# Lower probabilities times upper values on two column halves of TensorE, all eight key tiles of a half head in one stretch

## The chip, the cores and the metric

The kernel runs on one core of a Trainium2 chip. The metric is the device time of one execution in microseconds (us); lower is better. Before the change the median of three runs is 2208.74 us (2208.42 to 2209.5).

Engines are written as in the profile: PE is TensorE (PEld its weight loads), DVE VectorE, ACT ScalarE, POOL GpSimd, SP SyncE.

## The reference

Two layers, each an attention-and-convolution mixer followed by a gated feed-forward block, on one sequence of 1024 tokens with 1024 channels. The change lies in the attention of the mixer: 8 heads, queries and keys of 64 + 32 channels, values of 64 channels.

```
sc = (jnp.einsum("bqhd,bkhd->bhqk", qn, k_nope)
      + jnp.einsum("bqhr,bkr->bhqk", qr, k_rope))
p = jax.nn.softmax(sc.astype(jnp.float32) * scale, axis=-1).astype(v.dtype)
return jnp.einsum("bhqk,bkhd->bqhd", p, v)
...
u = a * jax.nn.sigmoid(gt)
u = _dwconv(u, w_dw_conv[l], b_dw_conv[l])
```

The second fragment is a depthwise convolution of 31 taps on 512 channels. The part of its taps that is left over when the attention begins (50 per layer) is computed beside the attention.

## The kernel before, in words

Attention is written out by hand in `attention` as a chain of 64 steps per layer (8 heads times 8 query tiles of 128), software-pipelined over steps. For step n TensorE's own order is:

- `values` (L1823): probabilities times values. A half head is 512 queries of one head; its 1024 keys are eight key tiles, and quarter c handles key tiles 2c and 2c+1 in one step. The four quarters of half head g stand in steps 4g+4 to 4g+7. The result `o` is one PSUM bank of 128 partitions by 512 queries.
- `turn(n)` (L1800 to L1803): eight 128x128 transposes on PE put a pair of finished probability tiles `p` into two PSUM banks `t`; ACT writes the upper part `pt` in f16 (L1802) and DVE the remainder, the lower part (L1803). So every half head has an upper and a lower `pt`.
- `scores(n+2)` (L1760): six matmuls into one of two double banks `s`; DVE takes the row maximum (L1762), and ACT the exponential (L1770, `expo(n+1)`, one step later) into `p`.

Values are also held as an upper and a lower f16 part, side by side in one weight tile of 128 columns (`v`, L1746 to L1749): for an even head columns 0 to 63 are the upper values (`main`) and 64 to 127 the lower ones (`aux`); for an odd head the other way round. One matmul of `pt` against that tile therefore yields upper values on 64 partitions of `o` and lower values on the other 64. After the last quarter ACT scales one half of `o` out of PSUM (L1829) and DVE adds the other half to it (L1830): the two halves are summed in any case.

In the step after a finished head `sums` (L1841) transposes eight columns of row sums on PE: a weight tile of 128 by 8, and DVE takes the reciprocals (L1843).

Beside this run the leftover taps (`tap_late`). `LATE_KINDS` (L83) gives each tap its kind, in a pattern of five that differs between the first and the second half of the list: `act` is two ACT instructions of half a tile (L1991), `pool` one product on POOL (L1994), and both then add through an accumulating DMA that POOL issues (L1999); `both` is a product and an addition on POOL (L1997). `LATE_COST` spreads the list over steps 0 to 56, each kind taking a share in proportion to its cost. When all taps are in, POOL sums the four channel blocks (L2005, `conv_total`), and ACT and DVE split the sum at the end (L2009, `conv_split`).

PE, DVE, ACT and POOL each execute their instructions in this written order.

Of the kernel before, what the change touches and what calls it, by code (L numbers as in the profile page):

```python
# [79 lines left out]
ROW_LATE = {0: (6,)}  # L80
E = mybir.EngineType
MANUAL = [E.PE, E.DVE, E.Activation, E.Pool, E.SP]
LATE_KINDS = (("act", "both", "pool", "act", "pool"), ("pool", "both", "pool", "pool", "pool"))  # L83
LATE_COST = {"act": 1.1, "pool": 3.5, "both": 4.8}
NEAR_TAPS = (12, 14, 15, 14)
NEAR_ORDER = (0, 1, 2, 3)
# [52 lines left out]
class Encoder:  # L139
# [1583 lines left out]
    def attention(self, l, u, conv, away, spill, kvs, loaded, ahead, wo, begun):  # L1723
        nc = self.nc
# [3 lines left out]
        state, v, vts = {}, [], {}  # L1728
# [79 lines left out]
        def values(group, c, n):  # L1808
            h, gg = divmod(group, 2)
            st = state[h]  # L1810
            e = h % 2
            main, aux = slice(e * 64, e * 64 + 64), slice(64 - e * 64, 128 - e * 64)
            if c == 0:
                if gg == 0 and e == 0:
                    st["y"], st["rb"] = self.blk(f"yt{l}_{h}"), self.blk(f"rb{l}_{h}")
                elif gg == 0:
                    st["y"], st["rb"] = state[h - 1]["y"], state[h - 1]["rb"]
                st["po", gg] = self.bank(f"o{l}_{h}_{gg}")
            y, rb, po = st["y"], st["rb"], st["po", gg] if c < 3 else st.pop(("po", gg))
            pt = st["pt"][gg][c // 2]  # L1820
            for s in range(2):
                for i in range(2):
                    nc.tensor.matmul(po, v[2 * c + i][:, h // 2, e, :], pt[s][:, 2 * (c % 2) + i, :],  # L1823
                                     start=(c == 0 and i == 0 and s == 0), stop=(c == 3 and i == 1 and s == 1))
            if c < 3:
                return
            st["pt"].pop(gg)
            qs = HALVES[gg]
            nc.scalar.activation(out=y[main, qs], in_=po[aux, :], func=AF.Copy, scale=vr[aux, 0:1])  # L1829
            nc.vector.scalar_tensor_tensor(out=y[main, qs], in0=po[main, :], scalar=vr[main, 0:1], in1=y[main, qs], op0=ALU.mult, op1=ALU.add)  # L1830
            if h < HEADS - 2 and gg:
                agenda[n + 1].append(lambda: sums(h, main, st, y, rb))
            elif h == HEADS - 1:
                if gg:
                    divide(y[main, qs], main, gg)
                else:
                    agenda[n + 1].append(lambda: (divide(y[main, qs], main, gg), finish(last, y, 0)))

        def sums(h, main, st, y, rb):
            pr = self.bank(f"sr{l}_{h}", (8, 128))  # L1840
            nc.tensor.transpose(pr, st["sums"], self.ident)  # L1841
            rs = self.cp.tile([8, 128], F32, name=f"rs{l}_{h}", tag="rs", bufs=2)
            nc.vector.reciprocal(out=rs, in_=pr)  # L1843
            nc.sync.dma_start(out=sd[h].rearrange("(a b) -> a b", a=8), in_=rs)
            nc.sync.dma_start(out=rb[main, :], in_=sd[h:h + 1].partition_broadcast(64))
            if h == HEADS - 2:
                for c, cs in enumerate(HALVES):
                    agenda[LAST_MULT[c]].append(lambda cs=cs: nc.vector.scalar_tensor_tensor(out=y[main, cs], in0=y[main, cs], scalar=1.0, in1=rb[main, cs], op0=ALU.mult, op1=ALU.mult))
            elif h % 2:
                agenda[h * 8 + 10 + Y_DELAY].append(lambda: nc.gpsimd.tensor_tensor(out=y, in0=y, in1=rb, op=ALU.mult))  # L1850
                agenda[h * 8 + 10 + Y_DELAY + (Y_SPLIT if h < 5 else Y_LAST)].append(
                    lambda: ys.append(self.split(y, f"ys{l}_{h}", on_pool=True)))
# [9 lines left out]
        def divide(ym, main, q):  # L1862
            nc.vector.tensor_tensor(out=ym, in0=inv[q][main, :], in1=ym, op=ALU.mult)
# [10 lines left out]
        def finish(h, y, c):  # L1874
            cs = HALVES[c]
            if c == 0:
                ys.append([self.blk(f"ys{l}_{h}{i}", F32R) for i in "hl"])
            hi, lo = (t[:, cs] for t in ys[-1])
            nc.scalar.copy(out=hi, in_=y[:, cs])
            nc.vector.scalar_tensor_tensor(out=lo, in0=y[:, cs], scalar=1.0, in1=hi.bitcast(F32), op0=ALU.mult, op1=ALU.subtract)  # L1880

        ys, inv, po = [], {}, begun["po"]
# [3 lines left out]
        while any(rest.values()):  # L1886
            j = max((j for j in rest if rest[j]), key=lambda j: (all(j != e for e, _ in late[-2:]), len(rest[j]), -j))
            late.append((j, rest[j].pop(0)))
        kinds = [LATE_KINDS[2 * i // len(late)][i % 5] for i in range(len(late))]
        costs, taken = [LATE_COST[kind] for kind in kinds], set()  # L1890
# [33 lines left out]
        for n in range(-2, total + 2):  # L1924
            if n == total - 2:
                expo(n + 1)
            for g, c in chain.get(n, ()):
                values(g, c, n)
# [9 lines left out]
            if n + 2 < total:  # L1938
                h, qt = divmod(n + 2, 8)
# [14 lines left out]
            if n == total:  # L1954
                values(2 * HEADS - 1, 0, n)
                values(2 * HEADS - 1, 1, n)
                early(1, range(2, 3))
                values(2 * HEADS - 1, 2, n)
                values(2 * HEADS - 1, 3, n)
# [180 lines left out]
```

## Time and profile before

| | |
|---|---|
| median of three runs | 2208.74 us |
| the profiled execution | 2208.39 us |
| its span, first to last instruction | 2206.6 us |
| granted TensorE clock | 0.999 |
| PE busy | 2196.8 us |
| DVE busy | 1831.5 us |
| ACT busy | 1468.9 us |
| POOL busy | 592.7 us |
| attention chain of layer 0 | about 210 to 409 us of the span |
| attention chain of layer 1 | about 1304 to 1503 us of the span |

Busy times are of the whole span; the attention chains are two stretches of about 200 us in which the balance between the engines is a different one. A matmul's recorded time runs from its start to its modelled end, and successive matmuls overlap, so what a matmul costs in a dense row is read from one start to the next.

### The profile page before, as it was taken

Reading aid. Unit: us, or ns where it says so; the run is one execution under the profiler, and the core shown is the slowest. Engines: PE = TensorE matmul, PEld = TensorE weight load, DVE = VectorE, ACT = ScalarE, POOL = GpSimd, SP = SyncE. Lnnn points to the kernel's source line nnn. Section 1 sums busy time; section 2 is a strip of 40 time slices with the busy share of each in tenths; the row PEclk is TensorE's granted clock in tenths of the full one; section 3 lists DMA queues with packets and bytes.
Section 4 is the critical chain, followed back from the end, with each engine's and each line's share of the span. In section 5 each row is a group of like instructions: output and inputs, shape, how many; then the busy total and the mean of one; then the engine's idle time right before and its main releaser. Section 6 shows DMA issues by size and latency. Waiting matters only on the chain.

```text
span 2206.6 us, 29859 instructions
## 1 busy us (share of the span) xinstructions
PE 2196.8 (100%) x10770; PEld 1320.0 (60%) x10770; DVE 1831.5 (83%) x2506; ACT 1468.9 (67%) x2207; POOL 592.7 (27%) x546
## 2 busy tenths in 40 slices
PE   9999999999999999999999999999999999999998
PEld 8887666784444444644488876667744444446445
DVE  7989888778988887787859788887798888878877
ACT  6455987746898886554623569786468887865544
POOL 1221799511121111000012227983111111110000
PEclk9999999999999999999999999999999999999999
DMA  6896887954588886554558968789646988856533
GB/s 193 165 176 176 167 166 156 289 141 115 137 243 257 223 258 155 191 170 155 167 134 168 192 151 176 154 182 237 169 104 143 258 240 241 239 142 218 183 116 120
DMA packets 163269, 400.96 MB, mean 182 GB/s; under 512 B 22144, under 2 KB 30192, under 8 KB 163120
## 3 DMA queue, kind: packets, MB, share of 16 engines
q0 software_dynamic: 67136, 154.28, 37.8%
q1 hardware_dynamic: 95696, 244.24, 32.5%
q8 instruction: 84, 1.38, 0.3%
q10 hardware_dynamic: 288, 0.53, 0.1%
q14 instruction: 65, 0.53, 0.1%
HBM read 270.75 MB, written 69.66 MB: 154 GB/s over the span
## 4 chain that ended last, share of the span: by engine, by line
PE 97%; DVE 1%; ACT 1%; issue 0%; DMA 0%; DVEq 0%; ACTq 0%
PE p L1251 36%; PE pd L1496 17%; PE po L985 7%; PE s L1760 7%; PE o L1823 5%; PE t L1800 5%; PE pq L239 3%; PE pa L239 3%; PE pg L239 2%; PE pkv L239 2%; PE pg L557 2%; PE pn L239 1%; PE pk L239 1%; PE pa L557 1%; PE pv L1736 1%; PE pu L239 1%
## 5 line engine op out<-in xcount | busy, mean ns | idle before, releaser
L1251 PE MATMUL p<-b,w 128*128 128x512 f16 x3696 | 804.0, 379 | 0.0
L1251 PEld LDWEIGHTS <-w 128*128 128x128 f16 x3696 | 361.6, 99 | 427.4 <-issue 1.1
L1496 PE MATMUL pd<-ab,wd 128*128 128x512 f16 (+2 forms) x1920 | 404.2, 373 | 0.0
L1142 POOL DMA_DIRECT2D wu<-in_w_up x176 | 152.6, 881 | 743.2 <-DVE w L1215 540.3
L1496 PEld LDWEIGHTS <-wd 128*128 128x128 f16 x1656 | 161.9, 98 | 179.4 <-issue 0.5
L1803 DVE SCALAR_TENSOR_TENSOR pt<-t,pt 128x512 f16<-128x512 f32 x256 | 163.8, 681 | 34.8 <-ACT pt L1802 33.7
L1760 PE MATMUL s<-k,q 96*128 96x512 f16 x768 | 186.9, 379 | 0.0
L1215 DVE SCALAR_TENSOR_TENSOR w<-wu,wf,w 128x512 f16<-128x512 f32 (+1 forms) x216 | 177.2, 834 | 3.9 <-ACT w L1212 3.9
L1994 POOL TENSOR_TENSOR late<-gate,par 128x1016 f32<-128x1016 f32 (+11 forms) x79 | 170.9, 2164 | 0.0
L1802 ACT ACTIVATE pt<-t 128x512 f16<-128x512 f32 x256 | 139.1, 597 | 45.9 <-PE t L1800 45.2
L1212 ACT ACTIVATE w<-wu,wf 128x512 f16<-128x512 f32 (+1 forms) x216 | 164.8, 781 | 0.1
L1762 DVE TENSOR_REDUCE mx<-s 128x1 f32<-128x1024 f32 x128 | 155.3, 1213 | 0.0
L1485 ACT ACTIVATE ab<-ac,ds 128x512 f16<-128x512 f32 x108 | 75.5, 716 | 108.5 <-DVE ac L1400 72.9
L1770 ACT ACTIVATE p<-s,mx 128x1024 f32<-128x1024 f32 x128 | 143.4, 1121 | 1.2 <-DVE mx L1762 0.8
L1977 DVE SCALAR_TENSOR_TENSOR conv<-gate,par,conv 128x1009 f32<-128x1009 f32 (+14 forms) x110 | 139.8, 1274 | 3.5 <-ACT conv L641 0.8
L1800 PEld LDWEIGHTS t<-ident,p 128*128 128x128 f32 x1024 | 120.0, 141 | 25.7 <-ACT p L1770 1.1
L1800 PE MATMUL t<-ident,p 128*128 128x128 f32 x1024 | 133.4, 273 | 0.6 <-ACT p L1770 0.6
L1823 PE MATMUL o<-pt,v 128*128 128x512 f16 x512 | 130.8, 379 | 0.0
L1708 DVE SCALAR_TENSOR_TENSOR o<-zg,par,o 128x1023 f32<-128x1023 f32 x88 | 112.7, 1281 | 8.9 <-ACT o L1702 7.4
L1259 DVE SCALAR_TENSOR_TENSOR zg<-p,wf,zg 128x512 f32<-128x512 f32 x72 | 54.0, 750 | 72.0 <-PE p L1251 62.3
L1760 PEld LDWEIGHTS <-q 96*128 96x128 f16 x768 | 74.1, 97 | 64.5 <-issue 2.1
L1708 DVE SCALAR_TENSOR_TENSOR v<-zv,par,v 128x1023 f32<-128x1023 f32 x88 | 112.1, 1276 | 0.0
(2173 smaller groups left out, 3936.7 us busy)
## 6 DMA issues: line engine op xcount, KB each, us to landing
wu<-in_w_up SPq DMA_DIRECT2D x98, 512.0 KB
wu<-in_w_up POOLq DMA_DIRECT2D x176, 256.0 KB, 4.8
sd<-in_w_down SPq DMA_DIRECT2D x44, 512.0 KB
ws<-sd SPq DMA_DIRECT2D x44, 512.0 KB
act<-v SPq DMA_DIRECT2D x36, 512.0 KB
ac<-act SPq DMA_DIRECT2D x72, 256.0 KB
wo<-in_w_o POOLq DMA_DIRECT2D x64, 256.0 KB, 7.4
x_mix<-y SPq DMA_DIRECT2D x32, 256.0 KB
```

The source lines that it names most:

```text
L239: nc.tensor.matmul(ps[:, HALVES[c]], w, x[:, HALVES[c]], start=(k == 0 and s == 0), stop=(k == n - 1 and s == 2))
L1212: nc.scalar.activation(out=t, in_=src, func=AF.Copy, scale=scale[f])
L1215: nc.vector.scalar_tensor_tensor(out=t, in0=src, scalar=scale[f], in1=hi, op0=ALU.mult, op1=ALU.subtract)
L1251: nc.tensor.matmul(ps, w[p][:, k * 128:(k + 1) * 128], b[:, q], start=(i in (1, 5, 2) and k == 0 and t == 0), stop=(k == 3 and t == 2), sk ...
L1496: nc.tensor.matmul(ps[t, m][:, cs], w[i, j][p][:, m * 128:(m + 1) * 128], b[:, q, cs], start=(i in (1, 5, 2) and j == 0 and s == 0), stop= ...
L1708: self.nc.vector.scalar_tensor_tensor(out=o[:, a:b], in0=z[:, at + a:at + b], scalar=self.par[l][:, tap:tap + 1], in1=o[:, a:b], op0=ALU.m ...
L1760: nc.tensor.matmul(ps[:, cs], q[0:96, i, qs], k[0:96, j, cs], start=(s == 0), stop=(s == 2))
L1762: nc.vector.tensor_reduce(out=mx, in_=ps, op=ALU.max, axis=AX.X, negate=True)
L1800: nc.tensor.transpose(tp[:, i, qi * 128:(qi + 1) * 128], st["p"][2 * qp + qi][:, kt * 128:(kt + 1) * 128], self.ident)
L1803: nc.vector.scalar_tensor_tensor(out=lo, in0=tp, scalar=P_SCALE, in1=hi, op0=ALU.mult, op1=ALU.subtract)
L1823: nc.tensor.matmul(po, v[2 * c + i][:, h // 2, e, :], pt[s][:, 2 * (c % 2) + i, :], start=(c == 0 and i == 0 and s == 0), stop=(c == 3 and ...
L1994: self.nc.gpsimd.tensor_tensor(out=p[:, lo:hi], in0=u[:, lo + s:hi + s], in1=self.tap(l, j, t).broadcast_to([128, hi - lo]), op=ALU.mult)
```

## The change

`values` no longer multiplies the lower probabilities in each quarter. Each quarter only has its two matmuls with the upper `pt` (both parts of the values). In the last quarter of a half head eight matmuls follow with the lower `pt`, one per key tile, and only with the upper values: 64 weight columns instead of 128. Even key tiles write partitions 0 to 63 of `o`, odd ones 64 to 127, that is, two halves of the array's columns in turn. The product of lower probabilities and lower values is left out. Separately, one of five taps in the second half of the list changes from POOL's product to ACT's.

```
-LATE_KINDS = (("act", "both", "pool", "act", "pool"), ("pool", "both", "pool", "pool", "pool"))
+LATE_KINDS = (("act", "both", "pool", "act", "pool"), ("act", "both", "pool", "pool", "pool"))
...
-            for s in range(2):
-                for i in range(2):
-                    nc.tensor.matmul(po, v[2 * c + i][:, h // 2, e, :], pt[s][:, 2 * (c % 2) + i, :],
-                                     start=(c == 0 and i == 0 and s == 0), stop=(c == 3 and i == 1 and s == 1))
+            for i in range(2):
+                nc.tensor.matmul(po, v[2 * c + i][:, h // 2, e, :], pt[0][:, 2 * (c % 2) + i, :],
+                                 start=(c == 0 and i == 0), stop=False, skip_group_check=True)
+            if c == 3:
+                for kt in range(8):
+                    rows = slice(kt % 2 * 64, kt % 2 * 64 + 64)
+                    nc.tensor.matmul(po[rows], v[kt][:, h // 2, e, main], st["pt"][gg][kt // 4][1][:, kt % 4, :],
+                                     start=False, stop=(kt >= 6), skip_group_check=True)
```

On PE, around the last quarter of the first half head (step 7 of layer 0), the order before is this; `pt_01` is the upper and `pt_11` the lower part of key tiles 4 to 7, and each matmul row stands twice, for two key tiles.

```order
L1760 MATMUL s_1_0_1902<-k_1_1686,q_1_1685 128x512
L1823 LDWEIGHTS v_6_1701
L1823 MATMUL o_0_0_1813<-pt_01_1715,v_6_1701 128x512
...
L1823 MATMUL o_0_0_1813<-pt_11_1716,v_6_1701 128x512
L1800 MATMUL t_0_30_1924<-ident,p_0_6_1876 128x128 x2
```

And now, at the same place; `pt_10` is the lower part of key tiles 0 to 3, `v_0` to `v_6` are the values of two key tiles each, and each matmul row stands twice here too.

```order
L1760 MATMUL s_1_0_1896<-k_1_1686,q_1_1685 128x512
L1822 MATMUL o_0_0_1813<-pt_01_1715,v_6_1701 128x512
L1827 LDWEIGHTS v_0_1593
L1827 MATMUL o_0_0_1813<-pt_10_1714,v_0_1593 64x512
L1827 MATMUL o_0_0_1813<-pt_10_1714,v_2_1616 64x512
L1827 MATMUL o_0_0_1813<-pt_11_1716,v_4_1667 64x512
L1827 MATMUL o_0_0_1813<-pt_11_1716,v_6_1701 64x512
L1800 MATMUL t_0_30_1921<-ident,p_0_6_1872 128x128 x2
```

Two full-width matmuls have gone from this step, and from the three steps before it, and eight of half the width have come in ahead of the transposes of this step.

On POOL, in the second half of the taps of layer 0, the order before is this (`late_j_t` is the product of tap t on channel block j):

```order
L1994 TENSOR_TENSOR late_0_26_2774<-gate_0_414,par_63 128x1013
L1999 DMA conv_0_473<-late_0_26_2774 128x1013
L1994 TENSOR_TENSOR late_1_26_2808<-gate_1_475,par_63 128x1013
L1997 TENSOR_TENSOR conv_1_537<-conv_1_537,late_1_26_2808 128x1013
L223 TENSOR_TENSOR ys_1l<-yt_0_1811,ys_1h 128x1024
```

And now on POOL:

```order
L2003 DMA conv_0_473<-late_0_26_2806 128x1013
L1998 TENSOR_TENSOR late_1_26_2845<-gate_1_475,par_63 128x1013
L2001 TENSOR_TENSOR conv_1_537<-conv_1_537,late_1_26_2845 128x1013
L223 TENSOR_TENSOR ys_1l<-yt_0_1811,ys_1h 128x1024
```

POOL keeps the DMA of tap 26 and loses its product, which stands on ACT now, as two halves behind the exponentials of two successive steps:

```order
L1770 ACTIVATE p_4_0_2804,sums_4_2754<-s_4_0_2755,mx_4_0_2762 128x1024
L1995 ACTIVATE late_0_26_2806<-gate_0_414,par_63 128x512
L1802 ACTIVATE pt_01_2713<-t_3_32_2811 128x2x256
...
L1770 ACTIVATE p_4_1_2841,sums_4_2754<-s_4_1_2795,mx_4_1_2802 128x1024
L1995 ACTIVATE late_0_26_2806<-gate_0_414,par_63 128x501
```

This happens to five taps per layer. Since the sum of the costs falls, the taps of the first half of the list spread over a few more steps than before.

## The prediction

> **What bounds the kernel now.** I read the page first: the shares of the engines and the chain that ended last.
>
> ```profile
> span 2206.6 us, 29859 instructions
> PE 2196.8 (100%) x10770; PEld 1320.0 (60%) x10770; DVE 1831.5 (83%) x2506; ACT 1468.9 (67%) x2207; POOL 592.7 (27%) x546
> ...
> PE 97%; DVE 1%; ACT 1%; issue 0%; DMA 0%; DVEq 0%; ACTq 0%
> ```
>
> PE is the bound on average, but the change touches only the two attention chains, so I read these by themselves: the stretches of layer 0 (columns: stretch, its length, then busy us and count of PE, PEld, DVE, ACT and POOL, granted clock, DMA share, GB/s).
>
> ```profile
> 230.00:260.00 30.00, 30.00 (x180) 18.63 (x179) 26.33 (x34) 27.96 (x51) 26.05 (x18) 1.00 0.85 169
> 260.00:290.00 30.00, 30.00 (x180) 18.66 (x179) 26.14 (x34) 26.58 (x49) 22.59 (x17) 1.00 0.95 192
> 290.00:320.00 30.00, 30.00 (x179) 18.40 (x178) 26.90 (x34) 24.07 (x43) 28.06 (x19) 1.00 0.73 141
> 320.00:350.00 30.00, 30.00 (x180) 18.48 (x178) 26.38 (x35) 23.38 (x42) 28.06 (x19) 1.00 0.81 159
> ```
>
> PE never idles there, at the full clock, so a matmul less is time less. But the cover is thin: DVE is at 88%, ACT at 93% in the first stretch, POOL at 94% in the last two. What I look for next is how a step is made up on PE, and then what a step costs the others.
>
> ```profile
> 267.69 1.03 PE L1800 MATMUL t<-ident,p 128*128 128x128 f32 x8
> 268.56 1.46 PE L1760 MATMUL s<-k,q 96*128 96x512 f16 x6
> 269.86 0.28 PE L1841 MATMUL sr<-ident,sums 128*8 128x128 f32 x1
> 269.97 1.02 PE L1823 MATMUL o<-pt,v 128*128 128x512 f16 x4
> 270.83 1.04 PE L1800 MATMUL t<-ident,p 128*128 128x128 f32 x8
> 271.71 1.46 PE L1760 MATMUL s<-k,q 96*128 96x512 f16 x6
> 273.00 1.03 PE L1823 MATMUL o<-pt,v 128*128 128x512 f16 x4
> 273.87 1.04 PE L1800 MATMUL t<-ident,p 128*128 128x128 f32 x8
> ```
>
> From start to start: six score matmuls 1.30 us, four value matmuls 0.865, eight transposes 0.87; a step is 273.87 - 270.83 = 3.04 us. One matmul of 512 columns costs 0.216 us, one transpose with its weight load 0.109.
>
> **The change, part by part.** *Removed:* per half head (four steps) 8 of 16 value matmuls: 8 x 0.216 = 1.73 us. They lie on the path, since PE is dense.
>
> *Added:* eight matmuls of half the columns, the stretch. No row of before has two matmuls on different halves of the array's columns, so I bound it. Each half still takes four matmuls of 512 queries in turn: not below 4 x 0.216 = 0.865 us. It takes no less by issue either: PE issues a load and a matmul every 0.109 us in the transposes, and 8 x 0.109 = 0.87. From above: if the halves take turns, 8 x 0.216 = 1.73 us; if in addition no weight load is hidden, 8 x (0.216 + 0.097) = 2.50 us, with the loads of the rows below. As for the first load of the second half, it can't be issued before the first half's matmul, so that half starts late by about one load. The narrow load of `sr` is the nearest row:
>
> ```profile
> L1841 PEld LDWEIGHTS sr<-ident,sums x14: 87/87/87, 245.1 to 1473.9; 128*8 128x8 f32 x14
> L1823 PEld LDWEIGHTS <-v x512: 95/98/101, 217.8 to 1502.3; 128*128 128x128 f16 x171
> L1760 PEld LDWEIGHTS <-q x768: 95/97/101, 200.2 to 1489.0; 96*128 96x128 f16 x192
> ```
>
> I take 0.865 + 0.087 = 0.95 us: in every row of before the load of the next matmul runs beside the present one, and nothing in them suggests that it would not when it goes to other columns. That both halves stream at once is the assumption on which the forecast stands. So a half head saves 1.73 - 0.95 = 0.78 us: three steps get shorter by 0.43 (to 2.60), the fourth longer by 0.52 (to 3.55), four steps together 11.36 instead of 12.14. With 32 half heads this is 32 x 0.78 = 24.9 us. The trace of the last half head is dense too, so I count it.
>
> A rule can be held against the 0.95. The Trainium skill, TensorE: Matmul & The Clock Gate, section Measured speedup vs the span model, gives 2.38 times for three column tiles. An estimate from it (the same 0.79 of ideal for two tiles, 1.59 times) makes the stretch 1.09 us and the saving 20.5 us; no run here shows it yet.
>
> *Entering and leaving the narrow form:* `sr` has 8 weight columns and stands between full-width matmuls in the rows above. It starts 1.30 us after the scores, as `o` does without it, and `o` follows 0.11 us later, the price of any transpose. So I cost the two switches per stretch at nothing; the other end is in the rivals.
>
> *Moved on PE:* the lower parts of quarters 0 to 2 are read up to three steps later, and those of quarter 3 behind four more matmuls. This removes waits for DVE's lower parts, none of which was on PE's path. The buffers of the next half head but one are first written two steps after the stretch, so nothing is late there.
>
> *The other engines in the shorter steps.* ACT, from rows of a plain step and of one with a tap and an eviction:
>
> ```profile
> 332.40 1.08 ACT L1802 ACTIVATE pt<-t 128x512 f16<-128x512 f32 x2 [0.86 <-PE t L1800]
> 333.37 1.12 ACT L1770 ACTIVATE p<-s,mx 128x1024 f32<-128x1024 f32 x1
> 334.37 0.21 ACT L1770 ACTIVATION_READ_ACCUMULATOR p<-s,mx 128x1 f32 x1
> ...
> 239.72 0.21 ACT L1770 ACTIVATION_READ_ACCUMULATOR p<-s,mx 128x1 f32 x1
> 239.81 0.73 ACT L1991 ACTIVATE late<-gate,par 128x506 f32<-128x506 f32 x1
> 240.56 0.69 ACT L1829 ACTIVATE yt<-o,sc 64x512 f32<-64x512 f32 x1
> 241.27 1.08 ACT L1802 ACTIVATE pt<-t 128x512 f16<-128x512 f32 x2
> ```
>
> Plain: 0.97 + 1.00 + 0.09 = 2.06 us; half a tap 0.73; the eviction 0.71. The first half of the list, 20 halves, spreads over about 26 steps now (56 x 70/152 by the cost table). ACT then needs 4 x 2.06 + 3.1 x 0.73 + 0.71 = 11.2 us per half head against PE's 11.36. The sum fits; a single step with a tap does not (2.79 against 2.60), so up to 3 x 0.19 = 0.57 us per half head can stall PE, in 13 half heads. DVE:
>
> ```profile
> 339.42 1.27 DVE L1803 SCALAR_TENSOR_TENSOR pt<-t,pt 128x512 f16<-128x512 f32 x2
> 340.62 1.20 DVE L1762 TENSOR_REDUCE mx<-s 128x1 f32<-128x1024 f32 x1
> 342.14 1.29 DVE L1803 SCALAR_TENSOR_TENSOR pt<-t,pt 128x512 f16<-128x512 f32 x2 [0.32 <-ACT pt L1802]
> 343.34 1.22 DVE L1762 TENSOR_REDUCE mx<-s 128x1 f32<-128x1024 f32 x1
> 344.48 0.94 DVE L1843 RECIPROCAL rs<-sr 8x128 f32<-8x128 f32 x1
> 345.34 1.23 DVE L1803 SCALAR_TENSOR_TENSOR pt<-t,pt 128x512 f16<-128x512 f32 x2
> ```
>
> Plain 1.20 + 1.20 = 2.40 us against 2.60; with the reciprocal 0.86 more, 3.26 against 2.71: up to 0.55 us in 14 steps. The stalls are thus between 0 and 13 x 0.57 + 14 x 0.55 = 15.1 us. PE works two steps ahead of the exponentials, and the long fourth step gives ACT and DVE 3.55 us to catch up, so I take values near the lower end: 0.2 and 0.1 us, 13 x 0.2 + 14 x 0.1 = 4.0 us.
>
> *`LATE_KINDS`:* per layer five products go from POOL to ACT.
>
> ```profile
> L1994 POOL TENSOR_TENSOR late<-gate,par 128x1016 f32<-128x1016 f32 (+11 forms) x79 | 170.9, 2164 | 0.0
> 391.52 2.68 POOL L2005 TENSOR_TENSOR lns<-lns,conv 128x1024 f32<-128x1024 f32 x1
> 405.23 1.05 ACT L2009 CAST lns0h<-lns 128x1024 fp32r<-128x1024 f32 x1
> ```
>
> POOL loses 5 x 2.16 = 10.8 us per layer, about what the chain gets shorter (12.5 - 2). Its sum `lns` was ready at 394.2 and read at 405.2: 11 us of cover, which stays. ACT gains 10 x 0.73 = 7.3 us in some 30 steps, 0.24 per step on top of 2.06 + 0.18 there, under 2.84: hidden. The accumulating DMAs stay as many; behind a slower one POOL alone queues, and its 11 us cover that. I cost this part at nothing. Without the cover it would be late by at most the 10.8 us that POOL keeps, twice.
>
> **Sum.** 2208.39 (the profiled execution, whose span is 2206.6) - 24.9 + 4.0 = 2187.5 us. That execution lies 0.35 us under the median of 2208.74, so for a median I say 2188.
>
> **Rivals.**
>
> 1. *ACT and DVE become the bound* in the attention. For it: 93% and 88% above, the steps of 2.79 and 3.26 us. Against it: both sums per half head fit, and every fourth step is long. With all 15.1 us of stalls: 2208.4 - 24.9 + 15.1 = 2198.6.
>
> 2. *Switching the array between full and half width empties it.* A matmul is recorded for 0.379 us where the next one starts after 0.216; waiting for its end costs 0.163, twice per stretch: 32 x 0.33 = 10.4 us, 2197.9 with the 4.0 us of stalls. The row of `sr` speaks against it. The Trainium skill, TensorEngine Tiling (Array Packing), section Key Properties, states that a change of tiling mode drains the engine; by that rule this rival holds, and the trace so far disagrees with it (0.11 us, no more than a transpose).
>
> 3. *The halves take turns*, loads hidden: the stretch is 1.73 us, nothing is saved: 2208 to 2209.
>
> 4. *Slower: the halves take turns and their loads are exposed*, because each load waits for the matmul before it. The stretch is 2.50 us, which adds 32 x 0.77 = 24.7: 2233. It is decided at a stretch of 1.73 us: anything longer loses. For it: no row shows two narrow matmuls in a row. Against it: the load of `sr` ran beside a matmul.
>
> The change doing what it says is not in doubt: the order on PE shows 64-row outputs that alternate.
>
> **How the numbers follow.** Forecast 2188 (its own range 2181 to 2193, the lower end from 0.865 us per stretch and no stalls: 2208.4 - 27.7): 0.50. Rival 1: 0.16. Rival 2: 0.10. Rival 3: 0.09. Rival 4: 0.15. A measurement of this kernel can tell about 0.2%, 4.4 us, from no change. Faster by more: 0.50 + 0.16 + 0.10 = 0.76; within: 0.09; slower: 0.15. A range from 2181 to 2210 takes in all but rival 4 and a sliver below.
>
> **What would show it.** Right: matmuls L1827 of the two halves start less than 0.11 us apart; from the first of them to the next transpose 0.9 to 1.1 us; plain steps of 2.60 us; PE's idle time in the chains a few us, put down to ACT `p` or DVE; a chain shorter by about 10 us per layer. Wrong: starts of L1827 0.216 us or more apart (rivals 3 and 4); a gap on both sides of the stretch (2); plain steps of 2.7 us or more with PE waiting for ACT (1); `lns` read later than the last value matmul (`LATE_KINDS`). The forecast fails above all if the two column halves don't stream at the same time.

## The result, and the profile after

The changed kernel takes 2195.61 us (median of 4 runs, 2195.24 to 2196.0) against 2208.7 us before: 13.1 us or 0.6% less, a ratio of 0.994 with a 95% interval of 0.9929 to 0.9952. The forecast of 2188 us was right in its sign; the gain is about two thirds of the 21 us that it promised, and the time lies 2.6 us above the range of 2181 to 2193 that the prediction gave for its own mechanism. The profiled execution took 2195.69 us. Line numbers behind the change are 4 higher than before (eviction L1833, `sr` L1845, half taps L1995, products L1998, accumulating DMAs L2003, `lns` L2009), and the full-width value matmuls are L1822.

The page of the changed kernel, same lines as before:

```profile
span 2193.9 us, 29880 instructions
PE 2182.6 (99%) x10770; PEld 1304.8 (59%) x10770; DVE 1828.8 (83%) x2506; ACT 1477.2 (67%) x2227; POOL 573.8 (26%) x536
...
PE 93%; ACT 4%; DVE 1%; issue 1%; DMA 0%; DVEq 0%; ACTq 0%
```

PE still carries the end, but ACT now holds 4% of the chain instead of 1%. The stretches of layer 0's attention (columns as before) say where:

```profile
230.00:260.00 30.00, 29.81 (x184) 17.98 (x183) 27.22 (x36) 28.57 (x52) 25.50 (x17) 1.00 0.86 164
260.00:290.00 30.00, 30.00 (x189) 17.91 (x188) 26.84 (x35) 27.78 (x51) 23.84 (x17) 1.00 1.00 199
290.00:320.00 30.00, 29.68 (x185) 18.06 (x184) 27.13 (x35) 26.33 (x49) 24.69 (x17) 1.00 0.71 146
320.00:350.00 30.00, 29.89 (x187) 17.75 (x185) 26.90 (x35) 25.78 (x47) 26.12 (x18) 1.00 0.92 189
```

ACT is at 95% in the first, and PE is no longer full in three of the four. What the stretch costs is read from PE's row of starts, in the timeline of PE in the changed kernel (start, length, instruction):

```profile
238.06 0.60 PE L1822 MATMUL o<-pt,v 128*128 128x512 f16 x2
238.59 1.05 PE L1827 MATMUL o<-pt,v 128*64 128x512 f16 x8
239.57 1.09 PE L1800 MATMUL t<-ident,p 128*128 128x128 f32 x8
240.50 1.46 PE L1760 MATMUL s<-k,q 96*128 96x512 f16 x6
241.80 0.60 PE L1822 MATMUL o<-pt,v 128*128 128x512 f16 x2
242.23 1.04 PE L1800 MATMUL t<-ident,p 128*128 128x128 f32 x8
243.11 1.46 PE L1760 MATMUL s<-k,q 96*128 96x512 f16 x6
244.40 0.28 PE L1845 MATMUL sr<-ident,sums 128*8 128x128 f32 x1
244.52 0.59 PE L1822 MATMUL o<-pt,v 128*128 128x512 f16 x2
244.95 1.36 PE L1800 MATMUL t<-ident,p 128*128 128x128 f32 x8
```

The step behind the stretch is a plain one, 242.23 - 239.57 = 2.66 us, of which 0.06 lies in its first transposes; the next eight transposes take 1.36 instead of 1.04. Three differences of starts make up the price of a stretch. From the two full value matmuls to the first narrow one it is 0.527 us instead of 2 x 0.216 = 0.432: **0.095**. From the first narrow one to the next transpose it is **0.985**, where four matmuls of 0.216 make 0.865. The transposes behind it take 0.93 instead of 0.87: **0.058**. Together 1.138 us where I had 0.95 and before had 1.73. All stretches in the steps agree to 0.01 us.

That the two halves stream at once is seen in the single records (start in us, engine, line), of which the grouped rows show only the first:

```
238.280  PE    L1822
238.585  PEld  L1827
238.587  PE    L1827
238.588  PEld  L1827
238.590  PE    L1827
238.827  PE    L1827
238.830  PE    L1827
239.042  PE    L1827
239.046  PE    L1827
239.258  PE    L1827
239.262  PE    L1827
239.569  PEld  L1800
239.572  PE    L1800
239.737  PE    L1800
```

Each pair starts 3 or 4 ns apart, and a pair follows a pair after 0.215 to 0.240 us, the price of one full matmul. But the first narrow load doesn't run beside the last full matmul: it starts 0.305 us behind its start, where the next full matmul would have begun at 0.216. The first full load behind the stretch does the same, 0.307 us behind the last narrow pair. The line's own summary has this as idle time of the weight loads (0.42 us each time, more than PE itself loses) that no other engine ends:

```profile
L1827 PEld LDWEIGHTS <-v x256: 106/110/110, 226.9 to 1489.4; 128*64 128x64 f16 x128
L1827 PE MATMUL o<-pt,v x256: 379/379/404, 226.9 to 1489.7; 128*64 128x512 f16 x128
its engine sat idle before it (us, times) until:
  issue: 13.6, 32
```

The second loss is the 1.36. ACT's timeline at the same place:

```profile
239.68 0.69 ACT L1833 ACTIVATE yt<-o,sc 64x512 f32<-64x512 f32 x1 [0.30 <-PE o L1827]
240.39 1.09 ACT L1802 ACTIVATE pt<-t 128x512 f16<-128x512 f32 x2
241.50 1.11 ACT L1770 ACTIVATE p<-s,mx 128x1024 f32<-128x1024 f32 x1
242.52 0.19 ACT L1770 ACTIVATION_READ_ACCUMULATOR p<-s,mx 128x1 f32 x1
242.61 0.71 ACT L1995 ACTIVATE late<-gate,par 128x506 f32<-128x506 f32 x1
243.22 1.07 ACT L1802 ACTIVATE pt<-t 128x512 f16<-128x512 f32 x2
244.17 1.12 ACT L1770 ACTIVATE p<-s,mx 128x1024 f32<-128x1024 f32 x1
245.17 0.21 ACT L1770 ACTIVATION_READ_ACCUMULATOR p<-s,mx 128x1 f32 x1
```

From the eviction on ACT has no free moment until its exponential and the sum behind it end at 245.38, and PE's third transpose of that step starts at 245.43. It is the second step behind the stretch, not the stretch itself, that is late. I call what eight transposes take from start to start above 0.873 us (0.93 right behind a stretch) their excess. It was 0.55 us per layer before and is 3.58 now, 6.1 us more in the two layers. About 5 us of these stand in the second step behind a stretch, 0.10 to 0.43 us there behind most of them; the rest is 0.27 and 0.30 us in two other steps of each layer. The table of waits names only a part of it, so it had to be read from the starts:

```profile
PE t L1800 <- ACT p L1770: 0.8, 3, 0.3
```

The account closes: 2208.39 - 32 x (1.73 - 1.138) + 6.1 = 2208.39 - 18.9 + 6.1 = 2195.6, against 2195.69 measured. So there are two things to test: what the price of a stretch hangs on, and what holds ACT up. `LATE_KINDS` is a third, since the account has nothing for it.

### The profile page after: what moved, and what is told of

Same layout as the page of the kernel before. It is cut to its first block, busy times and chain, and to the rows that moved or that the text cites. A ratio compares the mean times of both kernels' runs of the same rounds, so it can differ in the third digit from the quotient of the medians.

```text
span 2193.9 us, 29880 instructions
## 1 busy us (share of the span) xinstructions
PE 2182.6 (99%) x10770; PEld 1304.8 (59%) x10770; DVE 1828.8 (83%) x2506; ACT 1477.2 (67%) x2227; POOL 573.8 (26%) x536
## 4 chain that ended last, share of the span: by engine, by line
PE 93%; ACT 4%; DVE 1%; issue 1%; DMA 0%; DVEq 0%; ACTq 0%
PE p L1251 36%; PE pd L1496 17%; PE po L985 7%; PE s L1760 6%; PE t L1800 4%; PE pq L239 3%; PE pa L239 3%; PE pkv L239 2%; PE pg L239 2%; PE o L1822 2%; ACT p L1770 2%; PE pg L557 2%; PE pn L239 2%; PE o L1827 1%; ACT pt L1802 1%; PE pk L239 1%
## 5 line engine op out<-in xcount | busy, mean ns | idle before, releaser
L1998 POOL TENSOR_TENSOR late<-gate,par 128x1019 f32<-128x1019 f32 (+12 forms) x69 | 149.7, 2170 | 0.0
L1800 PE MATMUL t<-ident,p 128*128 128x128 f32 x1024 | 139.2, 276 | 2.0 <-ACT p L1770 0.8
L1158 ACT ACTIVATE wsq<-wu 128x1024 f16<-128x1024 f32 x88 | 92.1, 1047 | 9.8 <-DMA wu<-in_w_up 9.8
```

Of the source, the lines that this page charges most:

```text
L1800: nc.tensor.transpose(tp[:, i, qi * 128:(qi + 1) * 128], st["p"][2 * qp + qi][:, kt * 128:(kt + 1) * 128], self.ident)
```

## Experiments on the stretch

Theory 1 is that half-width matmuls pay only because both halves stream at once, and that each change of width has a price of its own. Its rival is that gathering eight matmuls in one stretch, or the width alone, does it.

**e1, the move alone.** The eight lower matmuls stand in one stretch, at full width.

```
-                    rows = slice(kt % 2 * 64, kt % 2 * 64 + 64)
-                    nc.tensor.matmul(po[rows], v[kt][:, h // 2, e, main], st["pt"][gg][kt // 4][1][:, kt % 4, :],
-                                     start=False, stop=(kt >= 6), skip_group_check=True)
+                    nc.tensor.matmul(po, v[kt][:, h // 2, e, :], st["pt"][gg][kt // 4][1][:, kt % 4, :],
+                                     start=False, stop=(kt == 7), skip_group_check=True)
```

> The eight lower matmuls stand in one stretch behind the last quarter as in the changed kernel, but at full width (128 columns, both parts of the values). Theory (the gain comes from two column halves that stream at once, and a switch between full and half width costs about 0.19 us per stretch): the stretch takes 8 x 0.216 = 1.73 us with no gap on either side, the chain is as long as before, 2208 to 2210 us. Rival (the gain comes from the new order, which takes lower parts off PE's path): about 2196 us, as the changed kernel.

Measured: 2215.81 us (2215.49 to 2216.58), 1.0033 times before (1.002 to 1.0046). PE's timeline in this kernel:

```profile
239.46 0.60 PE L1822 MATMUL o<-pt,v 128*128 128x512 f16 x2
239.90 1.89 PE L1826 MATMUL o<-pt,v 128*128 128x512 f16 x8
241.62 1.04 PE L1800 MATMUL t<-ident,p 128*128 128x128 f32 x8
```

There is no gap at full width: ten value matmuls in a row, up to the next transposes, take 2.16 us, 10 x 0.216. Yet neither expectation held. The transposes' excess is 8.2 us larger than before in the two layers together, and the two chains are 7.2 us longer, which is the loss (the median lies 7.1 us above that of before). PE has exactly the work of before; it is spread as three steps of 2.60 and one of 4.33 instead of four of 3.04. ACT and DVE have 2.06 and 2.40 us or more of work in each step and can't save up the long one. I put that down to the two double banks, which let PE's scores run no further ahead; no run here varies the banks.

**e2, one half only.** All eight narrow matmuls write partitions 0 to 63.

```
-                    rows = slice(kt % 2 * 64, kt % 2 * 64 + 64)
+                    rows = slice(0, 64)
...
-                                     start=False, stop=(kt >= 6), skip_group_check=True)
+                                     start=False, stop=(kt == 7), skip_group_check=True)
```

> As the changed kernel, but all eight narrow matmuls write partitions 0 to 63, so no two stand on different halves of the columns. Theory: they take turns at 0.216 us, the gaps on both sides of the stretch stay as they are: 32 x 0.865 = 27.7 us more than 2195.6, less the stalls that a longer stretch hides (up to 6 us): 2217 to 2223 us. Rival (a narrow matmul is cheaper by itself, whatever half it takes): about 2196 us.

Measured: 2222.74 us (2222.05 to 2223.36). PE's timeline in this kernel, the same stretch:

```profile
239.01 0.60 PE L1822 MATMUL o<-pt,v 128*128 128x512 f16 x2
239.54 1.91 PE L1827 MATMUL o<-pt,v 128*64 128x512 f16 x8
241.39 1.09 PE L1800 MATMUL t<-ident,p 128*128 128x128 f32 x8
```

From the first narrow matmul to the next transpose 1.845 us instead of 0.985: eight times 0.216, and the same 0.12 behind it; 0.53 ahead of it as well. The stretch alone moves the time by 32 x 0.86 = 27.5 us, and 2222.74 - 2195.61 is 27.1. This shows that the whole gain lies in the halves' running at once, and that the gaps come with the narrow form, whether or not the halves alternate.

**e3, a narrow pair in every quarter.** Nothing is gathered; there are 128 changes to the narrow form instead of 32.

```
-            if c == 3:
-                for kt in range(8):
+            if True:
+                for kt in (2 * c, 2 * c + 1):
```

> The narrow matmuls stand in their own quarters, one pair per step, so there are four switches to half width and back per half head in place of one. Theory: each further stretch costs 0.19 us, 3 x 32 x 0.19 = 18.2 us more than 2195.6, less up to 6 us of stalls since steps are even: 2208 to 2214 us. Rival (the gaps belong to the long stretch or to the eviction behind it, not to the switch): 2190 to 2196 us.

Measured: 2214.69 us (2214.45 to 2215.12). PE's timeline in this kernel:

```profile
260.63 1.46 PE L1760 MATMUL s<-k,q 96*128 96x512 f16 x6
261.93 0.60 PE L1822 MATMUL o<-pt,v 128*128 128x512 f16 x2
262.46 0.41 PE L1827 MATMUL o<-pt,v 128*64 128x512 f16 x2
262.79 1.09 PE L1800 MATMUL t<-ident,p 128*128 128x128 f32 x8
263.72 1.46 PE L1760 MATMUL s<-k,q 96*128 96x512 f16 x6
```

The price is there in every quarter: 0.53 ahead, 0.338 from the pair to the transposes instead of 0.216, and 0.93 for those, or 0.095 + 0.122 + 0.057 = 0.27 us for each time the width changes and changes back. A pair of narrow matmuls saves 0.216, so one pair doesn't pay and four do. The steps are even here (3.09 us), and the excess is back at that of before, 0.45 us per layer against 0.55: the unevenness, not the width, makes ACT late.

**e4, four quarters of the columns.** Sixteen matmuls of 32 weight columns, four at a time.

```
-                    rows = slice(kt % 2 * 64, kt % 2 * 64 + 64)
-                    nc.tensor.matmul(po[rows], v[kt][:, h // 2, e, main], st["pt"][gg][kt // 4][1][:, kt % 4, :],
-                                     start=False, stop=(kt >= 6), skip_group_check=True)
+                    for b in (0, 32):
+                        rows = slice(kt % 2 * 64 + b, kt % 2 * 64 + b + 32)
+                        nc.tensor.matmul(po[rows], v[kt][:, h // 2, e, e * 64 + b:e * 64 + b + 32], st["pt"][gg][kt // 4][1][:, kt % 4, :],
+                                         start=False, stop=(kt >= 6), skip_group_check=True)
```

> Each narrow matmul is cut into two of 32 columns, so sixteen matmuls go round the four column quarters; the computation is the same. Theory 1 (the gap belongs to the form with 64 columns; the transpose with 8 weight columns entered and left with no gap): the stretch is 0.95 us, 32 x 0.19 = 6 us less, 2189 to 2191 us. Theory 2 (every switch of a 16-bit matmul to fewer columns costs it): 2195 to 2197 us. If the four quarters did not stream at once: 2223 us or more.

Measured: 2196.03 us (2195.58 to 2196.12), the changed kernel's time. PE's timeline in this kernel:

```profile
238.48 0.60 PE L1822 MATMUL o<-pt,v 128*128 128x512 f16 x2
239.01 1.05 PE L1828 MATMUL o<-pt,v 128*32 128x512 f16 x16
239.99 1.09 PE L1800 MATMUL t<-ident,p 128*128 128x128 f32 x8
```

Sixteen take what eight took, 0.98 us, with the same gaps ahead and behind. So the price doesn't grow with the number of column groups; it is paid at the change.

## Experiments on what makes ACT late

Theory A: the half taps on ACT, in and behind the stretch's step, hold up its exponentials. Two rivals stand against it. Theory B: what counts is when POOL and its DMAs get their work. Theory D: DVE's chain of eviction, lower parts, maximum and reciprocal is the late one.

**e5, no ACT taps.** The 15 `act` taps per layer are left out, and with them their part of the convolution.

```
+            if kinds[i] == "act":
+                continue
```

> The changed kernel without the taps of kind act: their products on ACT and their accumulating DMAs are left out (15 of 50 taps per layer), all else stays. The changed kernel loses 6.1 us more than before in transposes that wait for an exponential, most of it in the second step behind a stretch. Theory A (ACT is the late one there: eviction, two upper parts, an exponential, half a tap, two upper parts and the next exponential follow the stretch without a break): the waits of 0.2 to 0.35 us fall to 0.1 or less, 4 us less, 2191 to 2192 us. Theory D (DVE's chain of eviction, lower parts, maximum and reciprocal is the late one): 2195 to 2196 us.

Measured: 2196.35 us (2195.94 to 2196.63), no gain. Inside the attention theory A holds: the transposes' excess falls from 3.58 to 1.47 us per layer. The time is lost ahead of it. DVE's timeline in this kernel, where the attention's queries are prepared:

```profile
194.84 5.48 DVE L780 SCALAR_TENSOR_TENSOR qns<-qn,qns 128x1024 f16<-128x1024 f32 x2
203.07 3.20 DVE L780 SCALAR_TENSOR_TENSOR qns<-qn,qns 128x1024 f16<-128x1024 f32 x1
```

And POOL's beside the second of these rows:

```profile
202.99 2.19 POOL L2000 TENSOR_TENSOR late<-gate,par 128x1019 f32<-128x1019 f32 x1
```

In the changed kernel the rows of 5.48 and 3.20 us are 2.42 and 1.23. POOL starts its products at 194.03 here; in the changed kernel it first waits 34.95 us for the first tap of ACT, issues that tap's DMA at 214.49 and starts its first product at 215.14. Beside POOL's work these results of DVE come later, and PE waits for DVE:

```profile
PE pv L1736 <- DVE v L1749: 1.5, 1, 1.5
PE s L1760 <- DVE qn L776: 1.5, 2, 0.8
```

So the run did not answer the question; it had taken away a wait that kept POOL off. Hence e9.

**e9, only the first ACT tap.** It holds POOL back as in the changed kernel; the other 14 `act` taps per layer are left out of the computation.

```
+            if i and kinds[i] == "act":
+                continue
```

> As the run without taps on ACT, but the first tap of the list stays on ACT, so that POOL waits for it and does not start its own taps beside DVE's work ahead of the attention; the other 14 taps of kind act per layer are left out. Theory A (the taps on ACT make the exponential late behind a stretch): T waits as in that run, about 4 us fewer than in the changed kernel, and nothing lost ahead of the attention: 2191 to 2192 us. If taking ACT's taps away does not help the whole, whatever the waits say: 2195 to 2196 us.

Measured: 2191.93 us (2191.71 to 2192.23), 3.7 us less than the changed kernel. PE's timeline in this kernel, the step in question:

```profile
244.83 1.04 PE L1800 MATMUL t<-ident,p 128*128 128x128 f32 x8
```

1.04 instead of 1.36. The excess falls from 3.58 to 1.58 us per layer, 4.0 us in all, against 3.8 us of span. Theory A is shown: of the 6.1 us, about 4 hang on the half taps; the rest, 0.10 us at every second stretch and 0.35 us near the end of each chain, stays without them. Theory D falls for these 4 us, since DVE's part in the attention is the same. The run also leaves out 14 accumulating DMAs per layer, but they are not needed for it: e6 and e12 below keep them, and 1.7 us of these waits in layer 1 of e6 and 2.5 us in e12 go there too. Nor does ACT work faster here: an exponential takes the same 1.12 us (median) before, in the changed kernel and here.

**e6, no half tap in a stretch's step.** The tap is put off to the next step.

```
-                while kinds[i] == "act" and n in taken:
+                while kinds[i] == "act" and (n in taken or n % 4 == 3):
```

> The changed kernel, but no half of a tap is put on ACT in the step of a stretch (it moves to the next free step), so that it no longer stands between the eviction and the second exponential behind the stretch. Nothing is left out. Theory A: the waits of 0.2 to 0.35 us fall to about 0.1, 3 us less, 2192 to 2193 us. Theory D: 2195 to 2196 us.

Measured: 2207.64 us (2205.73 to 2209.74), nearly all of the gain lost. The waits behind the stretches became short, as theory A has it (none or 0.10 us at most of them), and by the starts on PE the chain of layer 1 is 1.7 us shorter than in the changed kernel (199.8 instead of 201.5), with all its work still there. The whole loss lies in layer 0, whose chain is 12.9 us longer. There POOL, which issues the accumulating DMAs in its written order, now waited for ACT's later taps, and its `wo` loads behind the last tap left at 385.54 us instead of 372.46. The timelines of ACT and of PE in this kernel:

```profile
392.95 0.63 ACT L202 ACTIVATE wo<-wo 128x512 fp32r<-128x512 f32 x1 [12.97 <-DMA wo<-in_w_o]
```

```profile
394.97 1.01 PE L1822 MATMUL o<-pt,v 128*128 128x512 f16 x2 [11.72 <-ACT pt L1802]
```

ACT waits in order for `wo`, the upper parts wait behind that on ACT, and PE waits for those: one wait of 11.7 us, where the short ones that went were worth some 4 us. The granted clock was 0.83 in the 15 us behind it. So theory A holds for the steps, and for this placement theory B decides the time.

**e7 and e8, the eviction one step later**, alone and with e6's edit.

```
-            nc.scalar.activation(out=y[main, qs], in_=po[aux, :], func=AF.Copy, scale=vr[aux, 0:1])
-            nc.vector.scalar_tensor_tensor(out=y[main, qs], in0=po[main, :], scalar=vr[main, 0:1], in1=y[main, qs], op0=ALU.mult, op1=ALU.add)
+            def evict():
+                nc.scalar.activation(out=y[main, qs], in_=po[aux, :], func=AF.Copy, scale=vr[aux, 0:1])
+                nc.vector.scalar_tensor_tensor(out=y[main, qs], in0=po[main, :], scalar=vr[main, 0:1], in1=y[main, qs], op0=ALU.mult, op1=ALU.add)
+            if h < HEADS - 1:
+                agenda[n + 1].append(evict)
+            else:
+                evict()
```

> The changed kernel, but ACT and DVE take a half head's result out of PSUM at the end of the step behind the stretch instead of right behind it (the last head stays as it is). Theory A: this takes 0.71 us out of ACT's unbroken row and 0.67 us out of DVE's before the exponential that is waited for; all waits behind stretches vanish, 5 us less, about 2190 us, unless the bank that stays occupied longer makes the transposes wait. Theory D: the same, since DVE's eviction moves too. If the bank is short: 2196 us or more, with waits on ACT and DVE for the transposes' banks.

> Both edits at once: no half tap in the step of a stretch, and the eviction one step later. Theory A: 2189 to 2190 us (2195.6 less the 6 us of waits), no better than the later eviction by itself if that one removes them all. If neither edit touches the cause: 2195 to 2196 us.

Measured: 2220.96 us (2220.63 to 2224.21) and 2222.24 us (2221.86 to 2223.79), both slower than before the change. The waits of PE in e7's kernel:

```profile
PE t L1800 <- DVE yt L1836: 17.1, 14, 1.7
```

The transposes now wait for the last reader of `o`, up to 1.7 us at a time: with the eviction a step later, the PSUM bank that they are to be written into is still held. So a later eviction is no remedy here; whether the eviction adds to what makes ACT late, these two runs don't tell.

**e10 and e11, `LATE_KINDS`**: the changed kernel with the old pattern, and the kernel before with the new one.

```
-LATE_KINDS = (("act", "both", "pool", "act", "pool"), ("act", "both", "pool", "pool", "pool"))
+LATE_KINDS = (("act", "both", "pool", "act", "pool"), ("pool", "both", "pool", "pool", "pool"))
```

> The changed kernel with LATE_KINDS as before: five products per layer go back from ACT to POOL. By the prediction there are 11 us of cover on POOL (the sum of the channel blocks is ready 11 us before it is read) and ACT gets lighter by 7 us per layer: 2193 to 2196 us. Rival (POOL's own queue is tighter than that, since the loads of the output weights stand behind its taps and ACT waits for them, as happened when taps were moved later): 2200 us or more, with ACT waiting for the DMA of wo near the end of an attention.

> The kernel before with the new LATE_KINDS alone. With steps of 3.04 us ACT and POOL both have cover, so nothing changes: 2208 to 2210 us. If the extra half taps on ACT delay exponentials in even steps too: 2211 us or more.

Measured: e10 2199.56 us (2198.4 to 2202.38), 4.0 us above the changed kernel; e11 2208.53 us, 0.9999 times before (0.999 to 1.0009): nothing. POOL and ACT in e10's kernel at the end of layer 0's attention:

```profile
378.83 1.96 POOL L947 DMA_DIRECT2D wo<-in_w_o  x3
```

```profile
384.55 0.63 ACT L202 ACTIVATE wo<-wo 128x512 fp32r<-128x512 f32 x1 [4.48 <-DMA wo<-in_w_o]
```

And in the changed kernel, without a wait:

```profile
372.46 1.95 POOL L947 DMA_DIRECT2D wo<-in_w_o  x3
```

```profile
380.31 0.64 ACT L202 ACTIVATE wo<-wo 128x512 fp32r<-128x512 f32 x1
```

And in the kernel before:

```profile
377.35 1.96 POOL L947 DMA_DIRECT2D wo<-in_w_o  x3
```

```profile
386.39 0.64 ACT L202 ACTIVATE wo<-wo 128x512 fp32r<-128x512 f32 x1
```

It is the chain of e6 again, smaller: POOL's taps, `wo` loads, ACT, and 3.2 us on PE. Before, the first load landed 5.6 us after its issue, at about 382.9, and was read at 386.39: 3.5 us of cover, and the shorter steps take more than that. So the edit alone is worth nothing, and with the shorter steps about 4 us: it pays for what the shorter chain takes from POOL's cover. All of this is in layer 0, where the chain of e10 is 4.6 us longer than in the changed kernel; in layer 1 nothing waits for `wo`, the transposes' excess is 0.8 us smaller and the chain 0.8 us shorter.

**e12, the taps spread by what this showed.** Half taps moved to the list's second half, where ACT had more room, begun one step earlier, and none in a stretch's step.

```
-LATE_KINDS = (("act", "both", "pool", "act", "pool"), ("act", "both", "pool", "pool", "pool"))
+LATE_KINDS = (("act", "both", "pool", "pool", "pool"), ("act", "both", "pool", "act", "pool"))
...
+            n = max(n - (kinds[i] == "act"), 0)
...
-                while kinds[i] == "act" and n in taken:
+                while kinds[i] == "act" and (n in taken or n % 4 == 3):
```

> The changed kernel with its taps placed by what e5, e6 and e9 showed: the same count of ACT taps, but two of five in the second half of the list and one of five in the first (the two patterns change places); a tap's first half may start one step earlier, and no half tap stands in a step that holds a stretch. Theory A (6.1 us of the changed kernel's PE idle time come from ACT being late in the second step behind a stretch, when a half tap stands in the stretch's step beside the eviction): the transposes' excess falls to about 0.1 us per stretch, about 1.5 to 1.9 us per layer instead of 3.1 or so, and the time to 2192 (2191 to 2194). Theory B (what counts is when POOL gets its products from ACT: with the half taps kept out of some steps POOL ends its taps later, the loads of wo behind them come late and ACT waits for them at the first evictions of the layer's next part): 2197 or more, with waits of ACT for DMA wo of several us.

Measured: 2193.51 us (2193.17 to 2193.95), 0.9931 times before (0.9918 to 0.9945), and 2.1 us below the changed kernel; the fastest of the kernels here that compute everything the changed one does. The time is as theory A has it. The transposes' excess falls by 2.5 us in the two layers, as the span does (2191.4 after 2193.9), though less than expected: 2.6 and 2.1 us per layer remain instead of 1.5 to 1.9. The `wo` loads leave in time, at 372.43 us.

## Why the prediction was right, and where it was off

- *PE is the bound, so a matmul less is time less*: right; the account by starts on PE closes to 0.1 us. But the measured 2195.61 us lies outside the forecast's own range and nearer to the times of rival 2 (2197.9) and rival 1 (2198.6): parts of both mechanisms ran beside the one that was forecast, and only the wider range, which was spread over the rivals, holds the result.
- *Both halves stream at once*: right, by the pairs' starts and by e2 (27.1 us without it). Rivals 3 and 4 fall. Two parts of the working were wrong without harm: the second half doesn't start a load (0.087 us) late but 3 ns, and issue at 0.109 us per load and matmul is no floor, since in e4 sixteen follow one another in four groups 0.216 to 0.226 us apart. That the late start of 0.087 us stood in the sum was luck: it paid for a third of the price of the next step.
- *Entering and leaving the narrow form costs nothing*: **this is the step that failed**. It is 0.095 in and 0.12 + 0.058 out, 0.27 us per stretch, 8.7 us in all. Less the 0.087 us that I had put in for the late half and that isn't there, the stretch is 0.19 us dearer than forecast, and 24.9 us of saving becomes 18.9: 6.0 of the 8.1 us by which the sum of 2187.5 lay too low. I let one row, `sr`, speak for every narrow load. It still stands in the changed kernel without a gap (0.113 us to the next matmul), but it is an f32 transpose of 8 columns, while this is an f16 matmul of 64. Which of the differences exempts it was not tried and stays open.
- *Rival 2* was thus right that every switch has a price, and nearly in its size: 0.33 us per stretch forecast, 0.27 measured. The sign that I had named for it, a gap on both sides, is there. The rule of the Trainium skill, TensorEngine Tiling (Array Packing), section Key Properties, that a change of tiling mode drains the engine, agrees with the gaps of e2, e3 and e4, about 0.27 us each time. A wait for the whole of a matmul's recorded end it is not, since the load starts 0.305 us after the matmul's start and the record, whose end is modelled, is 0.377 long. What PE waits for in the gap stays open.
- *The stretch by the speedup of three tiles*: the estimate of 1.09 us from the Trainium skill, TensorE: Matmul & The Clock Gate, section Measured speedup vs the span model, was nearer to 1.138 than mine. But e3 and e4 show no share lost in each matmul: one pair and four pairs pay the same 0.27 us per change of width and back, so a longer stretch pays less per matmul.
- *Stalls of 4.0 us*: 6.1 measured, inside my bounds of 0 and 15.1; that is the other 2.1 us. The two errors go the same way and add up. Rival 1's mechanism runs at about two fifths of its price. The place was wrong. I expected the long fourth step to let ACT catch up; e1 shows that gathering the work in one step in four costs 8 us of stalls by itself, with no matmul saved, and e3 that even steps have no more than before.
- *Moved on PE* at nothing: wrong for the same reason. I had looked for buffers that come late and not at the steps that get uneven.
- *`LATE_KINDS` at nothing, under 11 us of cover*: right as a sum for the kernel as it is, by wrong reasoning. The reader I looked at (`lns`, 11 us) isn't the tight one. That is ACT, which reads `wo`, queued behind the same taps on POOL, with about 3.5 us of cover, and e10 shows 4 us lost without the edit. My sign for it, `lns` read late, would not have shown this.
- *A chain shorter by about 10 us per layer*: 6.4 (half of the 12.7 us of span).

## What to carry to other kernels

Narrow matmuls on separate column groups really run at once, but each change of width and back cost 0.27 us here, so gather enough of them to pay for it (one pair of 512 columns was too few, four were enough). Gathering makes steps uneven, and an engine with little slack could not bank the long step here: move its side work with the stretch, or keep the steps even. Before a cover is trusted, follow everything queued behind the engine that gets less time, to its tightest reader.

## What the runs showed of the hardware beyond that

- Four column groups start within about 10 ns of one another (e4), and 16 weight loads of 92 to 97 ns were done in 0.55 us: loads for different column groups overlap too.
- DVE's f16 results `qns` that started while POOL ran a product or a sum took 2.15 to 3.40 us instead of 1.22 (e5, five of them in the two layers). Each ended 1.08 to 1.09 us behind the end of that POOL instruction, as 203.07 + 3.20 = 206.27 us does behind 202.99 + 2.19 = 205.18. So it looks as if DVE had waited for POOL to finish; the run doesn't tell what they share, and a `qn` result out of PSUM at 200.25 kept its 1.21 us beside a product.
- A gap on PE can cost more than itself. In e10 PE stands still for 3.24 us before 386.56, and the clock granted from 385.5 to 392 us is 0.50, some 2 us after PE's last matmul ended at 383.3: from start to start the next eight transposes take 1.71 us instead of 0.87 and the six scores behind them 2.56 instead of 1.30. The profiled execution is 4.6 us longer than the changed kernel's although its other stalls are smaller. In e6 the clock is 0.50 from 386.5 to 400 us, some 3 us after PE stopped for 11.7 us. In e7, whose 14 waits are at most 1.7 us long, the mean clock of layer 0's attention is 1.00. That the gap lowers the clock is thus read from the order in time; no run tests it. These 15 us in e10:

```profile
380.00:395.00 15.00, 11.76 (x60) 7.03 (x60) 8.19 (x12) 9.82 (x18) 14.40 (x11) 0.77 1.06 280
```

In the same 15 us of the changed kernel PE is busy for 14.87 us at a clock of 1.00.
